# A DeltaNet mixer's triangular substitution moved from GpSimd to VectorE, with the projections around it put in another order

## The chip, the cores and the metric

The kernel runs on one core of a Trainium2 chip. The metric is the device time of one execution in microseconds (us), the median of three runs. Engines are named as the profile names them: PE is TensorE's matmul and PEld its weight load, DVE is VectorE, ACT is ScalarE, POOL is GpSimd, SP is SyncE, whose queue issues nearly all DMAs.

## The reference

Two trunk layers of width 1024 work on 384 tokens, 128 of a prompt and 256 of a sample. Layer 0 mixes by two head groups side by side, HGRN2 and gated DeltaNet, 4 heads of 128 each and both directions; layer 1 is neighbourhood attention. Each layer ends with a squared-ReLU MLP, and every part has an adaptive shift, scale and gate ("modulation"). The part of layer 0's mixer that matters here, cut:

```python
q_a, f_fw, f_bw, i_a, g_a, qkv_b, g_b, a_fw, a_bw, b_fw, b_bw = _split(h @ w_in, _AB_SIZES)
qa = _heads(jax.nn.silu(q_a), H_A).astype(f32) * DK_A ** -0.5
f = lbh + (1.0 - lbh) * jax.nn.sigmoid(_heads(f_raw, H_A).astype(f32))      # HGRN2's gate
qkv = jax.nn.silu(_short_conv(qkv_b, conv_w))                               # DeltaNet: 5 taps
qb = _l2norm(...) * DK_B ** -0.5 ; kb = _l2norm(...)
# _gated_delta_chunked, per chunk:
kb = k * beta[..., None]
A = jnp.where(strict, jnp.einsum('bhntd,bhnsd->bhnts', kb, k) * L, 0.0)     # L: decays
T = jnp.eye(CHUNK, dtype=A.dtype) + A
u = lax.linalg.triangular_solve(T, v * beta[..., None], left_side=True, lower=True, unit_diagonal=True)
w = lax.linalg.triangular_solve(T, kb * jnp.exp(g)[..., None], left_side=True, lower=True, unit_diagonal=True)
attn = jnp.where(tri, jnp.einsum('bhntd,bhnsd->bhnts', q, k) * L, 0.0)
```

The kernel takes whole tiles of 128 tokens as DeltaNet's chunks. It inverts T: first the 32 x 32 blocks on the diagonal by substitution, then two doubling levels (32 to 64 to 128) by matmuls.

## The kernel before, in words

Tokens lie in three tiles of 128. Each fp32 product is made of three matmuls: a weight half is loaded ("raw", a ring of 3), rounded by ACT ("whi", 4), and its rest ("wlo", 4) subtracted by DVE, or by POOL for the halves that the table `ON_POOL` names (`split_w`, L210). The input projection is done in blocks of 256 columns, each of two such halves: f (HGRN2's forget gates), q (its queries), v (its values), c (what DeltaNet's conv takes), g (output gates). A block of f, q, c or g is 48 matmuls (L645 to L647), one of v 72 (L687 to L689).

The order of the program comes from a string, `STEPS`: letters name a block, or so many steps of three generators: h is HGRN2 (seven doubling levels over three tiles, each a round over PE, ACT and DVE), d is DeltaNet's levels, a is the modulation (loads "adr", two slots, and 4 matmuls a step). A scheduler then takes the instructions of the whole program, estimates when each could run, and fixes the order on each engine; an engine runs its list strictly in that order. The table `ORDER` with `behind()` can pin an instruction behind another that was marked. Tiles come from rings: when a ring is full, whoever next takes a slot waits until its last reader is done. The ring "sm4" has five slots.

DeltaNet before the levels: `gdn_prep` makes, for each tile and direction, the products of the keys, times the decays (L997), into `NT_`, and 24 copies (L1000) take the diagonal blocks out of it. `gdn_solve` transposes these (L1030, L1035), weights them by cd = beta/|k|^2 (L1033), and sends them through DRAM (L1038, L1039, L1043) to a layout with one block in each of 96 partitions. There the substitution runs on POOL: 31 steps, each a product (L1052) and a subtraction (L1053). The inverses go back (L1055, L1057), are transposed (L1059), and written into the diagonal of `NT_` by 8 copies (L1074). The levels multiply by cd where they need it (L1091, L1120).

Also touched: `evac_q` (L705, L706: query times its sigmoid), `evac_f` (L714, L715: the gate), `evac_conv` (first tap L933, four more L935, then a sum on POOL, L943, and a transpose on PE, L949), `gdn_attn` (L1010), HGRN2's first products (L746, L747), its mask (L748) and its levels (L757, L762, L769, L771, L780, L783).

Of the kernel before, what the change touches and what calls it, by code (L numbers as in the profile page):

```python
# [48 lines left out]
}  # L49
# [6 lines left out]
d f3 f1 f2 d q1 a2 q0 d h a2 h a h c4 h a d h3 d c5 h a2 d h v0 h d h d v1 a d h3  # L56
c0 h3 c1 h5 d2 h d2 h d h7 g0 g1 d m g2 g3 a3
# [7 lines left out]
ON_POOL = {1: (0, 1), "c5": (0,), "q0": (0,)}  # L65
# [41 lines left out]
class Trunk:  # L107
# [525 lines left out]
    def fm_block(self, src, hh, evac, key):  # L633
# [6 lines left out]
        for g in range(2):  # L640
            with self.behind(key, g):
                for n in range(2):
                    c = slice(n * P, (n + 1) * P)
                    for k in range(g * 4, g * 4 + 4):
                        nc.tensor.matmul(pg[n], whi(k)[:, c], hhi[:, k], start=(k == 0), stop=False)  # L645
                        nc.tensor.matmul(pg[n], whi(k)[:, c], hlo[:, k], start=False, stop=False)  # L646
                        nc.tensor.matmul(pg[n], wlo(k)[:, c], hhi[:, k], start=False, stop=(k == KT - 1))  # L647
# [29 lines left out]
    def tm_half(self, src, hh, evac):  # L677
# [3 lines left out]
        whi, wlo = self.split_w(self.slab(src.rearrange("(k p) n -> p k n", p=P), KT, 256), KT, 256)  # L681
        for t0, n in ((0, 2), (2, 1)):
            pg = self.ps([P, 2, 256], "acc")[:, 0:n]
            for t in range(t0, t0 + n):
                c = slice(t * P, (t + 1) * P)
                for k in range(KT):
                    nc.tensor.matmul(pg[:, t - t0], hhi[:, k, c], whi(k), start=(k == 0), stop=False)  # L687
                    nc.tensor.matmul(pg[:, t - t0], hlo[:, k, c], whi(k), start=False, stop=False)
                    nc.tensor.matmul(pg[:, t - t0], hhi[:, k, c], wlo(k), start=False, stop=(k == KT - 1))  # L689
# [39 lines left out]
    def hgrn_tile(self, t, Q, K):  # L729
# [17 lines left out]
        nc.vector.tensor_mul(Q[:, 1], q, G[:, 0])  # L747
# [102 lines left out]

# [71 lines left out]
    def evac_conv(self, n):  # L922
# [4 lines left out]
        def f(pg):  # L927
# [5 lines left out]
            nc.vector.tensor_scalar(acc, raw[:, 0:386], w(0), None, op0=ALU.mult)  # L933
# [23 lines left out]
    def gdn_scalars(self):  # L957
        nc = self.nc
        c = lambda n: self.mixc([P, NT, 4], n)
        s, r2 = c("knorm"), c("kr2")  # L960
# [8 lines left out]
        bc = lambda x: x.unsqueeze(2).broadcast_to([P, NT, 2, 4])
        nc.vector.tensor_mul(self.cv, dh(self.beta), bc(s))  # L970
        nc.vector.tensor_mul(self.cd, dh(self.beta), bc(r2))
        nc.vector.tensor_mul(self.cs, self.cd, dh(self.eg))

    def block(self, j):
        return self.blocks[:, j].rearrange("p (d t h c) -> p d t h c", d=2, t=NT, h=4)

    def gdn_prep(self):

        nc = self.nc
        self.NT_ = self.m12([P, NT, 2, 4, P])  # L980
        self.AT_ = self.m12([P, NT, 2, 4, P])
        self.NC = self.block(0)
        b4 = lambda x: x.unsqueeze(1).broadcast_to([P, 4, P])
        for t in range(NT):
# [3 lines left out]
            for d in range(2):  # L988
# [8 lines left out]
                nc.vector.tensor_mul(self.NT_[:, t, d], pk, L)  # L997
                for b in range(4):
                    r = slice(32 * b, 32 * b + 32)
                    nc.vector.tensor_copy(self.NC[r, d, t], self.NT_[r, t, d, :, r])  # L1000

    def gdn_attn(self):

        nc = self.nc
# [18 lines left out]

    def gdn_solve(self):

        nc = self.nc
# [12 lines left out]
        nc.sync.dma_start(s1[:, 1], N3)  # L1039
        A = self.sm4([96, 32, 32])  # L1040
        sy = lambda s, b: s[32 * b:32 * b + 32].rearrange("i d (m j) -> (d m) i j", j=32)
        for b in range(4):
            nc.sync.dma_start(A[24 * b:24 * b + 24], sy(s1, b))  # L1043
# [4 lines left out]
        e = nc.gpsimd
        for j in range(31):
            m, w = 31 - j, j + 1  # L1050
            t = pr.rearrange("p i j -> p (i j)")[:, :m * w].rearrange("p (i j) -> p i j", j=w)
            e.tensor_tensor(t, A[:, w:, j:j + 1].broadcast_to([96, m, w]), X[:, j:j + 1, :w].broadcast_to([96, m, w]), op=ALU.mult)  # L1052
            e.tensor_tensor(X[:, w:, :w], X[:, w:, :w], t, op=ALU.subtract)  # L1053
# [767 lines left out]
```

## Time and profile before

| | us |
|---|---|
| three runs | 1140.26, 1137.22, 1137.5 |
| median | 1137.5 |
| profiled execution, own time | 1139.19 |
| its span in the profile | 1137.3 |
| its mean granted TensorE clock | 0.983 |
| TensorE busy in the span | 1081.7 (95%) |
| VectorE, ACT, POOL busy | 762.3, 485.1, 277.2 |

Busy times are sums over the span. In rows of a timeline the first number is the start, the second the duration; in groups the numbers after the bar are the sum and the mean in ns, then the idle time before them and what ended it. Line numbers are those of the kernel in question; those of the changed kernel are larger by three up to about line 960, and L210 becomes L213, L739 L742, L748 L751.

### The profile page before, as it was taken

To read this page: it belongs to the slowest core of one execution; us is meant where nothing else is said; L and a number is where in the kernel's file an instruction comes from. 1 tells how busy PE (TensorE), PEld (TensorE's weight loads), DVE (VectorE), ACT (ScalarE), POOL (GpSimd) and SP (SyncE) were. 2 spreads that over 40 slices of the span, in tenths; PEclk is the share of its full clock that TensorE was granted. 3 is DMA by queue.
4 is the path that set the end of the run, shared out by engine and by line. 5 is a ranking of instruction groups with operands and counts; after the bars stand their busy time and mean duration, and the time that the engine had idled before them with its cause. 6 is when DMAs were issued, how large, how long until landed. Compare 5 with 4: busy or idle time off the path is not lost.

```text
span 1137.3 us, 17975 instructions
## 1 busy us (share of the span) xinstructions
PE 1081.7 (95%) x6853; PEld 937.8 (82%) x6853; DVE 762.3 (67%) x1188; ACT 485.1 (43%) x874; POOL 277.2 (24%) x295
## 2 busy tenths in 40 slices
PE   6989969999998999999999999999988999999998
PEld 3868857988986898888889788888668889998987
DVE  3678499995467698968887654878748773333333
ACT  4464333342445543433334444656636433333330
POOL 0054894231204011111112252324012011111102
PEclk9989989999998999999999999999989999999999
DMA  8953725333162687766674147566425764433301
GB/s 290 292 168 107 220 79 162 129 108 110 38 218 78 244 275 261 260 202 222 226 248 134 41 101 211 153 185 167 119 74 184 281 203 130 133 126 126 99 38 56
DMA packets 142091, 184.66 MB, mean 162 GB/s; under 512 B 36803, under 2 KB 113685, under 8 KB 142005
## 3 DMA queue, kind: packets, MB, share of 16 engines
q1 hardware_dynamic: 141685, 183.44, 51.0%
q8 instruction: 54, 0.88, 0.3%
q14 instruction: 32, 0.26, 0.1%
q10 hardware_dynamic: 320, 0.07, 0.0%
HBM read 171.53 MB, written 4.61 MB: 155 GB/s over the span
## 4 chain that ended last, share of the span: by engine, by line
PE 74%; DVE 7%; DMA 6%; POOL 6%; issue 2%; SPq 2%; ACT 2%; POOLq 0%; DVEq 0%; ACTq 0%
PE acc L1340 7%; PE acc L1341 7%; PE acc L1342 7%; PE tmp L1355 7%; PE tmp L1356 7%; PE tmp L1354 7%; POOL sm L1053 2%; POOL sm L1052 2%; PE po L1731 2%; DMA ada<-in_ada_w 2%; PE acc L646 2%; PE acc L645 2%; PE acc L647 1%; PE acc L672 1%; PE acc L673 1%
## 5 line engine op out<-in xcount | busy, mean ns | idle before, releaser
L210 DVE TENSOR_TENSOR wlo<-raw,whi 128x1024 fp32r<-128x1024 f32 x192 | 238.0, 1250 | 167.2 <-ACT whi L209 145.5
L209 ACT ACTIVATE whi<-raw 128x1024 fp32r<-128x1024 f32 x198 | 205.9, 1050 | 335.0 <-PE acc L1342 190.6
L1374 POOL TENSOR_TENSOR h<-h 128x384 f32<-128x384 f32 x56 | 69.5, 1242 | 424.9 <-ACT h L1371 423.7
L1341 PE MATMUL acc<-wlo,h 128*128 128x512 f32 x380 | 148.5, 391 | 0.1
L1340 PE MATMUL acc<-whi,h 128*128 128x512 f32 x380 | 146.0, 393 | 0.6 <-issue 0.6
L346 DVE SCALAR_TENSOR_TENSOR adc<-adr,scz,adc 128x1024 f32<-128x1024 f32 x98 | 128.5, 1342 | 10.3 <-DMA adr<-in_ada_w 10.1
L1342 PE MATMUL acc<-whi,h 128*128 128x512 f32 x380 | 121.2, 391 | 0.0
L1340 PEld LDWEIGHTS acc<-whi,h 128*128 128x128 f32 x380 | 71.2, 188 | 20.6 <-ACT whi L209 5.0
L1355 PE MATMUL tmp<-hyA,whi 128*128 128x384 f32 (+1 forms) x256 | 85.1, 333 | 2.2 <-DVE hyA L565 2.2
L1354 PE MATMUL tmp<-hyA,whi 128*128 128x384 f32 (+1 forms) x256 | 84.1, 334 | 3.0 <-DVE hyA L564 3.0
L1354 PE MATMUL tmp<-hyB,whi 128*128 128x384 f32 (+1 forms) x256 | 83.8, 329 | 1.2 <-DVE hyB L564 1.2
L1356 PE MATMUL tmp<-hyA,wlo 128*128 128x384 f32 (+1 forms) x256 | 84.8, 332 | 0.0
L1355 PE MATMUL tmp<-hyB,whi 128*128 128x384 f32 (+1 forms) x256 | 84.0, 329 | 0.7 <-DVE hyB L565 0.7
L1341 PEld LDWEIGHTS acc<-wlo,h 128*128 128x128 f32 x380 | 71.4, 188 | 14.3 <-DVE wlo L210 0.5
L1342 PEld LDWEIGHTS acc<-whi,h 128*128 128x128 f32 x380 | 71.0, 188 | 13.7
L1356 PE MATMUL tmp<-hyB,wlo 128*128 128x384 f32 (+1 forms) x256 | 82.1, 328 | 0.0
L645 PE MATMUL acc<-hyA,whi 128*128 128x384 f32 x208 | 74.1, 356 | 0.0
L646 PE MATMUL acc<-hyA,whi 128*128 128x384 f32 x208 | 71.4, 343 | 0.0
L647 PE MATMUL acc<-hyA,wlo 128*128 128x384 f32 x208 | 71.0, 342 | 0.0
L1375 DVE TENSOR_TENSOR h<-h,h 128x384 fp32r<-128x384 f32 (+2 forms) x72 | 37.8, 526 | 40.6 <-POOL h L1374 39.8
L1354 PEld LDWEIGHTS tmp<-hyA,whi 128*128 128x128 f32 x256 | 48.7, 191 | 4.4 <-ACT km L560 3.4
L1355 PEld LDWEIGHTS tmp<-hyA,whi 128*128 128x128 f32 x256 | 49.3, 192 | 3.3 <-DVE hyA L565 2.4
(454 smaller groups left out, 2357.7 us busy)
## 6 DMA issues: line engine op xcount, KB each, us to landing
raw<-in_w_mlp SPq DMA_DIRECT2D x128, 512.0 KB, 3.8
adr<-in_ada_w SPq DMA_DIRECT2D x80, 512.0 KB, 4.7
raw<-in_w_in_ab SPq DMA_DIRECT2D x34, 512.0 KB, 4.7
ada<-in_ada_w SPq DMA_DIRECT2D x32, 256.0 KB, 5.5
raw<-in_w_qkv_na SPq DMA_DIRECT2D x32, 256.0 KB, 3.8
raw<-in_w_out_ab SPq DMA_DIRECT2D x8, 512.0 KB, 4.5
m<-gs SPq DMA_DIRECT2D x8, 512.0 KB
raw<-in_w_qkv_na SPq DMA_DIRECT2D x8, 512.0 KB
```

The costliest lines, as they stand in the source:

```text
L209: self.nc.scalar.activation(hi, x, AF.Copy)
L210: (eng or self.nc.vector).tensor_tensor(lo, x, hi.bitcast(F32), op=ALU.subtract)
L346: nc.vector.scalar_tensor_tensor(acc[v], raw, s[v], acc[v], op0=ALU.mult, op1=ALU.add)
L645: nc.tensor.matmul(pg[n], whi(k)[:, c], hhi[:, k], start=(k == 0), stop=False)
L646: nc.tensor.matmul(pg[n], whi(k)[:, c], hlo[:, k], start=False, stop=False)
L647: nc.tensor.matmul(pg[n], wlo(k)[:, c], hhi[:, k], start=False, stop=(k == KT - 1))
L1340: nc.tensor.matmul(pg, shi, w2hi(n)[:, o], start=start, stop=False)
L1341: nc.tensor.matmul(pg, shi, w2lo(n)[:, o], start=False, stop=False)
L1342: nc.tensor.matmul(pg, slo, w2hi(n)[:, o], start=False, stop=last)
L1354: nc.tensor.matmul(pg[n], w1hi(k)[:, c], hhi[:, k, tc_], start=(k == 0), stop=False)
L1355: nc.tensor.matmul(pg[n], w1hi(k)[:, c], hlo[:, k, tc_], start=False, stop=False)
L1356: nc.tensor.matmul(pg[n], w1lo(k)[:, c], hhi[:, k, tc_], start=False, stop=(k == KT - 1))
```

## The change

The substitution's 62 operations run on VectorE, over 112 partitions (one direction in partitions 0 to 47, the other from 64). One direction's blocks are turned end for end by a copy with a negative stride ahead of it, and turned back behind it. The diagonal blocks are fetched by DMA straight from `NT_` (four to DRAM, eight from there) and the inverses written by DMA straight back into it (eight to DRAM, one for the levels, four into `NT_`): 25 DMAs where 11 were. The 24 and the 8 copies, two transposes and two products by cd are gone. The keys' products take cd at once: 24 operations of 128 x 128 (`weigh`) for 6 of 128 x 512, in `gdn_prep` and again in `gdn_attn`; the products by cd in the levels become ACT copies, and the small vectors cv and cs are replaced by 1/|k|, eg and cu. The query's product goes to POOL (behind an ACT copy), the gate and the conv's first tap go to ACT. More halves are split on POOL: half of q1, both of v0 and v1, half of c4 (before: half of c5 and of q0). In `STEPS` the queries and values stand right behind the gates, ahead of HGRN2; an "a!" is pinned behind the block ahead of it, HGRN2's levels behind the substitution, and the transpose of the inverses behind HGRN2's first products. The last modulation steps are pinned behind the last gate block.

On POOL, the stretch around the substitution, before (wlo is a split half, sm tiles are of the ring sm4, km is HGRN2's 1 - f):

```order
L996 TENSOR_TENSOR m_121_750<-m_121_750,tri 128x512 x4
L210 TENSOR_TENSOR wlo_1282<-raw_1277,whi_1281 128x1024
L1046 MEMSET sm_139_846 96x1024
L1047 MEMSET sm_139_846 96x32
L1052 TENSOR_TENSOR sm_140_847<-sm_138_841,sm_139_846 96x31
L1098 MEMSET sm_203_1345 32x12x32
L1098 MEMSET sm_207_1391 32x12x32
L1053 TENSOR_TENSOR sm_139_846<-sm_139_846,sm_140_847 96x31
L1052 TENSOR_TENSOR sm_140_847<-sm_138_841,sm_139_846 96x60
```

and now:

```order
L1103 MEMSET sm_236_1626 32x12x32
L742 TENSOR_TENSOR km_1491<-x 128x512
L742 TENSOR_TENSOR km_1514<-x 128x512
L742 TENSOR_TENSOR km_1537<-x 128x512
L213 TENSOR_TENSOR wlo_1308<-raw_1303,whi_1307 128x1024
L213 TENSOR_TENSOR wlo_1312<-raw_1305,whi_1311 128x1024
L1103 MEMSET sm_240_1672 32x12x32
L710 TENSOR_TENSOR hyB_647<-hyB_647,cv_1209 128x3x128
L710 TENSOR_TENSOR hyB_647<-hyB_647,cv_1213 128x3x128
L213 TENSOR_TENSOR wlo_1404<-raw_1399,whi_1403 128x1024
L710 TENSOR_TENSOR hyB_647<-hyB_647,cv_1287 128x3x128
L213 TENSOR_TENSOR wlo_1408<-raw_1401,whi_1407 128x1024
```

wlo_1308 and wlo_1312 are the halves of the first value block, wlo_1404 and wlo_1408 those of the second. The second L1103 takes the sixth tile of a ring of five; the first of the five is the matrix A that the substitution reads (sm_137 below). On VectorE, around HGRN2's first products, before:

```order
L706 TENSOR_TENSOR hyB_647<-cv_1342,acc_1290 128x3x128
L746 TENSOR_TENSOR hq_1437<-hyB_647,m_102_649 128x512
L747 TENSOR_TENSOR hq_1437<-hyB_647,m_102_649 128x512
L746 TENSOR_TENSOR hq_1438<-hyB_647,m_102_649 128x512
L747 TENSOR_TENSOR hq_1438<-hyB_647,m_102_649 128x512
L746 TENSOR_TENSOR hq_1439<-hyB_647,m_102_649 128x512
L747 TENSOR_TENSOR hq_1439<-hyB_647,m_102_649 128x512
L748 TENSOR_TENSOR hyB_647<-hg_1443,eye 128x4x32
```

and now, from the substitution's last step:

```order
L1059 TENSOR_TENSOR sm_140_827<-sm_137_824,sm_139_826 112x31
L1060 TENSOR_TENSOR sm_139_826<-sm_139_826,sm_140_827 112x31
L1053 COPY sm_138_825<-sm_139_826 48x1024
L749 TENSOR_TENSOR hq_1487<-hyB_647,m_102_649 128x512
L750 TENSOR_TENSOR hq_1487<-hyB_647,m_102_649 128x512
L749 TENSOR_TENSOR hq_1488<-hyB_647,m_102_649 128x512
L750 TENSOR_TENSOR hq_1488<-hyB_647,m_102_649 128x512
L749 TENSOR_TENSOR hq_1489<-hyB_647,m_102_649 128x512
L750 TENSOR_TENSOR hq_1489<-hyB_647,m_102_649 128x512
L1207 STREAM_TRANSPOSE hyB_645<-hyB_645 128x768
L213 TENSOR_TENSOR wlo_1727<-raw_1720,whi_1726 128x1024
L213 TENSOR_TENSOR wlo_1909<-raw_1904,whi_1908 128x1024
```

HGRN2's first products, which stood behind the query's, now stand behind the whole substitution, and its first level behind four operations of DeltaNet's (L1115) and later halves:

```order
L213 TENSOR_TENSOR wlo_2383<-raw_2378,whi_2382 128x1024
L1115 TENSOR_SCALAR m_120_747<-gd_1644 32x12x32
L938 SCALAR_TENSOR_TENSOR cv_1782<-cr_652,prm,cv_1782 128x386
L1115 TENSOR_SCALAR m_120_747<-gd_1658 32x12x32
L938 SCALAR_TENSOR_TENSOR cv_1782<-cr_652,prm,cv_1782 128x386 x2
L1115 TENSOR_SCALAR m_120_747<-gd_1690 32x12x32
L213 TENSOR_TENSOR wlo_2387<-raw_2380,whi_2386 128x1024
L938 SCALAR_TENSOR_TENSOR cv_1782<-cr_652,prm,cv_1782 128x386
L1115 TENSOR_SCALAR m_120_747<-gd_1704 32x12x32
L774 COPY_PREDICATED hyB_647<-lv,hg_1818 128x4x32
```

L774 is the first level's masked copy. The diff, cut:

```diff
+    ("step", "!"): ["block"],
+    "hgrn": ["solve"],
+    "solved": ["hq"],
 STEPS = """
-d f3 f1 f2 d q1 a2 q0 d h a2 h a h c4 h a d h3 d c5 h a2 d h v0 h d h d v1 a d h3
-c0 h3 c1 h5 d2 h d2 h d h7 g0 g1 d m g2 g3 a3
+f3 a! f1 f2 a! q1 a! q0 a! v0 a! v1 h3 d2! a! d c4 h a! d h c5 h a! d h3 d h d h a! d2 h3
+c0 h3 c1 h5 d2 h d2 h d h7 g0 g1 d m g2 g3 a3!
-ON_POOL = {1: (0, 1), "c5": (0,), "q0": (0,)}
+ON_POOL = {1: (0, 1), "q1": (0,), "q0": (0,), "v0": (0, 1), "v1": (0, 1), "c4": (0,)}
     def evac_q
-            nc.vector.tensor_mul(self.qa[:, :, h], s, pv)
+            nc.scalar.activation(self.qa[:, :, h], pv, AF.Copy)
+            nc.gpsimd.tensor_tensor(self.qa[:, :, h], self.qa[:, :, h], s, op=ALU.mult)
     def evac_f
-            nc.vector.tensor_scalar(self.G[:, :, d, h], s, self.lb1[:, h:h + 1], self.lb[:, h:h + 1],
-                                    op0=ALU.mult, op1=ALU.add)
+            nc.scalar.activation(self.G[:, :, d, h], s, AF.Identity, scale=self.lb1[:, h:h + 1], bias=self.lb[:, h:h + 1])
     def evac_conv
-            nc.vector.tensor_scalar(acc, raw[:, 0:386], w(0), None, op0=ALU.mult)
+            nc.scalar.activation(acc, raw[:, 0:386], AF.Copy, scale=w(0))
     def gdn_prep
-                nc.vector.tensor_mul(self.NT_[:, t, d], pk, L)
-                for b in range(4):
-                    r = slice(32 * b, 32 * b + 32)
-                    nc.vector.tensor_copy(self.NC[r, d, t], self.NT_[r, t, d, :, r])
+                self.weigh(self.NT_[:, t, d], pk, L, t, d)
+    def weigh(self, out, pk, L, t, d):
+        for h in range(4):
+            self.nc.vector.scalar_tensor_tensor(out[:, h], pk[:, h], self.cd[:, t, d, h:h + 1], L[:, h], op0=ALU.mult, op1=ALU.mult)
+    def diagonal(self, b):
+        r = slice(32 * b, 32 * b + 32)
+        return self.nt[r].rearrange("p d t h c -> p d (t h) c")[:, :, :, r]
     def gdn_solve
...
+        A, A0 = self.sm4([P, 32, 32]), self.sm4([P, 32, 32])
+        X = self.sm4([P, 32, 32])
+        pr = self.sm4([P, 32, 32])
...
+        for b in range(4):
+            nc.sync.dma_start(s1[rows(b)], self.diagonal(b))
+        for d, x in enumerate((A0, A)):
+            for b in range(4):
+                nc.sync.dma_start(x[part(b, d)], blocks(s1, b, d))
...
+        reverse(A, A0)
+        e, n = nc.vector, 112
         for j in range(31):
...
+            e.tensor_tensor(t, A[:n, w:, j:j + 1].broadcast_to([n, m, w]), X[:n, j:j + 1, :w].broadcast_to([n, m, w]), op=ALU.mult)
+            self.mark["solve"] = e.tensor_tensor(X[:n, w:, :w], X[:n, w:, :w], t, op=ALU.subtract)
+        reverse(A0, X)
+        for d, x in enumerate((A0, X)):
+            for b in range(4):
+                nc.sync.dma_start(blocks(s2, b, d), x[part(b, d)])
+        nc.sync.dma_start(XC, s2)
         for b in range(4):
+            nc.sync.dma_start(self.diagonal(b), s2[rows(b)])
     def gdn_levels
-            nc.vector.tensor_mul(pb[T], p[T], cd[T].broadcast_to([32, NT, 4, 32]))
+            nc.scalar.activation(pb[T], p[T], AF.Copy)
     def gdn_steps
+        with self.behind("solved"):
+            nc.vector.transpose(self.blocks[:, 1], self.blocks[:, 0])
```

More of the change, by code (lines that the diff above doesn't have):

```diff
@@ L646, in fm_block @@
                         nc.tensor.matmul(pg[n], whi(k)[:, c], hlo[:, k], start=False, stop=False)
-                        nc.tensor.matmul(pg[n], wlo(k)[:, c], hhi[:, k], start=False, stop=(k == KT - 1))
+                        self.mark["block"] = nc.tensor.matmul(pg[n], wlo(k)[:, c], hhi[:, k], start=False, stop=(k == KT - 1))
         for n in range(2):
@@ L675, in tm_parts, with tm_half @@
         return part
-    def tm_half(self, src, hh, evac):
+    def tm_half(self, src, hh, evac, pool=()):
         nc = self.nc
         hhi, hlo = hh
-        whi, wlo = self.split_w(self.slab(src.rearrange("(k p) n -> p k n", p=P), KT, 256), KT, 256)
+        whi, wlo = self.split_w(self.slab(src.rearrange("(k p) n -> p k n", p=P), KT, 256), KT, 256, pool=pool)
         for t0, n in ((0, 2), (2, 1)):
@@ L688, in tm_half @@
                     nc.tensor.matmul(pg[:, t - t0], hlo[:, k, c], whi(k), start=False, stop=False)
-                    nc.tensor.matmul(pg[:, t - t0], hhi[:, k, c], wlo(k), start=False, stop=(k == KT - 1))
+                    self.mark["block"] = nc.tensor.matmul(pg[:, t - t0], hhi[:, k, c], wlo(k), start=False, stop=(k == KT - 1))
             evac(t0, n, pg)
@@ L794, in hgrn_steps @@
             for x in g:
-                next(x)
+                with self.behind("hgrn"):
+                    next(x)
                 yield
@@ new lines, in gdn_solve @@
+        s1 = self.dp.tile([P, 2, 12, 32], F32, tag="s1", name="s1")
+        s2 = self.dp.tile([P, 2, 12, 32], F32, tag="s2", name="s2")
+        rows = lambda b: slice(32 * b, 32 * b + 32)
+        blocks = lambda s, b, d: s[rows(b), d].rearrange("i m j -> m i j")
+        part = lambda b, d: slice(64 * d + 12 * b, 64 * d + 12 * b + 12)
+        for b in range(4):
+            nc.sync.dma_start(s1[rows(b)], self.diagonal(b))
+        for d, x in enumerate((A0, A)):
+            for b in range(4):
+                nc.sync.dma_start(x[part(b, d)], blocks(s1, b, d))
@@ L1053, in gdn_solve @@
-            e.tensor_tensor(X[:, w:, :w], X[:, w:, :w], t, op=ALU.subtract)
-        for b in range(4):
-            nc.sync.dma_start(sy(s2, b), X[24 * b:24 * b + 24])
-        XC = self.block(0)
-        nc.sync.dma_start(f(XC), s2.rearrange("p d c -> p (d c)"))
-        XD = self.block(1)
-        nc.vector.transpose(f(XD), f(XC))
-        self.Xc = (XC[:, 0], XD[:, 1])
-        self.XTc = (XD[:, 0], XC[:, 1])
+            t = flat(pr)[:n, :m * w].rearrange("p (i j) -> p i j", j=w)
+            e.tensor_tensor(t, A[:n, w:, j:j + 1].broadcast_to([n, m, w]), X[:n, j:j + 1, :w].broadcast_to([n, m, w]), op=ALU.mult)
@@ new lines, in gdn_solve @@
+            self.mark["solve"] = e.tensor_tensor(X[:n, w:, :w], X[:n, w:, :w], t, op=ALU.subtract)
+        reverse(A0, X)
+        XC, XD = (self.blocks[:, j].rearrange("p (d m c) -> p d m c", d=2, c=32) for j in range(2))
+        for d, x in enumerate((A0, X)):
+            for b in range(4):
+                nc.sync.dma_start(blocks(s2, b, d), x[part(b, d)])
+        nc.sync.dma_start(XC, s2)
+        for b in range(4):
+            nc.sync.dma_start(self.diagonal(b), s2[rows(b)])
+        self.Xc = [XD[:, d].rearrange("p (t h) c -> p t h c", t=NT) for d in range(2)]
@@ L1069, in gdn_levels @@
         N = XT = self.NT_
-        cd = self.cd[:, :, d].unsqueeze(3)
         tag = "gd"
-        for b in range(4):
-            r = slice(32 * b, 32 * b + 32)
-            nc.vector.tensor_copy(XT[r, :, d, :, r], self.XTc[d][r])
         first = lambda o, L: slice(o, o + L)
@@ L1474, in layer0 @@
         for step in STEPS.split():
-            kind, n = step[0], int(step[1:] or 1)
+            kind, n = step[0], int(step[1:].strip("!") or 1)
             if kind in chains:
                 for _ in range(n):
-                    next(chains[kind], None)
+                    with self.behind("step", step[-1]):
+                        next(chains[kind], None)
             elif kind == "f":
```

68 lines of the change are left out of this document (24 added, 44 removed).

## The prediction

> **What bounds the kernel now.** I began with the page: who is busy, where TensorE's clock is low, and which chain ended last.
>
> ```profile
> span 1137.3 us, 17975 instructions
> PE 1081.7 (95%) x6853; PEld 937.8 (82%) x6853; DVE 762.3 (67%) x1188; ACT 485.1 (43%) x874; POOL 277.2 (24%) x295
> ...
> PE 74%; DVE 7%; DMA 6%; POOL 6%; issue 2%; SPq 2%; ACT 2%; POOLq 0%; DVEq 0%; ACTq 0%
> ```
>
> TensorE is busy for 95% of the span; only its idle time and low clock can be won. POOL's 6% of the last chain is the substitution. The windows show where the mixer loses time (columns: PE, PEld, DVE, ACT, POOL busy, then PE's granted clock, DMA share, GB/s).
>
> ```profile
> 100.00:160.00 60.00, 51.44 (x453) 43.95 (x452) 42.15 (x52) 22.47 (x31) 43.28 (x51) 0.96 0.54 172
> 160.00:265.00 105.00, 99.71 (x1245) 87.57 (x1245) 94.67 (x160) 38.30 (x68) 43.45 (x56) 0.97 0.44 134
> 150.00:160.00 10.00, 5.00 (x78) 4.54 (x79) 10.00 (x12) 2.74 (x4) 9.37 (x11) 0.78 0.34 105
> 160.00:170.00 10.00, 8.61 (x139) 7.00 (x139) 10.00 (x13) 3.31 (x6) 9.37 (x10) 0.88 0.16 46
> ```
>
> From 100 to 265 us PE is idle 8.56 + 5.29 = 13.85 us and loses 0.04 x 51.44 + 0.03 x 99.71 = 5.05 us to the clock. VectorE (DVE) is itself busy 90% from 160 to 265. The waits of TensorE name two causes:
>
> ```profile
> PE tmp L949 <- POOL cv L943: 5.4, 2, 3.1
> ...
> PE hg L757 <- DVE hyB L748: 2.8, 1, 2.8
> PE hg L757 <- DVE hyB L771: 2.4, 2, 1.4
> ```
>
> L949 waits for POOL, where the conv's L943 stands in line with the substitution; L757 waits for HGRN2's levels on VectorE. The substitution's ends:
>
> ```profile
> 112.95 2.10 SPq L1043 DMA_DIRECT2D sm<-s  x4
> 117.38 0.25 POOL L1052 TENSOR_TENSOR sm<-sm,sm 96x31 f32<-96x31 f32 x1 [5.71 <-DMA sm<-s]
> 180.30 0.58 POOL L1053 TENSOR_TENSOR sm<-sm,sm 96x31 f32<-96x31 f32 x1
> 189.53 1.60 PE L1086 MATMUL gd<-hyB,m 32*32 32x32 f32 x48
> ```
>
> It runs from 117.4 to 180.9 (63.5 us), and DeltaNet's first level follows at 189.5.
>
> **The substitution moves.** Durations for VectorE and POOL, by group and from the timeline:
>
> ```profile
> L210 DVE TENSOR_TENSOR wlo<-raw,whi 128x1024 fp32r<-128x1024 f32 x32 | 42.9, 1347 | 24.2 <-ACT whi L209 19.8 <-PE ada L326 4.2
> L780 DVE TENSOR_TENSOR hq<-hq,m 128x512 f32<-128x512 f32 x21 | 17.9, 851 | 0.0
> L1000 DVE COPY hyB<-m 32x128 f32<-32x128 f32 x24 | 7.3, 304 | 0.4
> L997 DVE TENSOR_TENSOR m<-hg,m 128x512 f32<-128x512 f32 x6 | 4.1, 685 | 0.1
> L815 DVE SCALAR_TENSOR_TENSOR m<-hq,m,hg 128x128 f32<-128x128 f32 x8 | 2.2, 343 | 2.7 <-PE hg L836 2.7
> ...
> L210 POOL TENSOR_TENSOR wlo<-raw,whi 128x1024 fp32r<-128x1024 f32 x3 | 7.9, 2618 | 12.0 <-ACT whi L209 12.0
> L739 POOL TENSOR_TENSOR km<-x 128x512 f32<-128x512 f32 x3 | 3.8, 1274 | 0.0
> ...
> 91.61 0.18 DVE L971 TENSOR_TENSOR cd<-beta,kr 128x24 f32<-128x24 f32 x1
> 91.83 1.29 DVE L972 TENSOR_TENSOR cs<-cd,eg 128x24 f32<-128x24 f32 x1
> 95.73 1.30 POOL L996 TENSOR_TENSOR m<-m,tri 128x512 f32<-128x512 f32 x1 [0.19 <-ACT m L995]
> 134.27 1.10 POOL L1052 TENSOR_TENSOR sm<-sm,sm 96x231 f32<-96x231 f32 x1
> 134.81 3.44 DVE L747 TENSOR_TENSOR hq<-hyB,m 128x512 f32<-128x512 f32 x1
> 135.33 2.38 POOL L210 TENSOR_TENSOR wlo<-raw,whi 128x1024 fp32r<-128x1024 f32 x1
> ```
>
> Start: the keys' weighting is now 24 x 343 ns = 8.2 us where 24 copies and 6 products took 11.4, and its last piece can follow POOL's mask, which ended at 97.03: 97.03 + 4 x 0.343 = 98.4. SyncE then issues four DMAs and, behind one weight load, eight. By the row of four (issued from 112.95, landed before 117.38: 4.4 us, of which 2.1 is issue): first stage, issued at about 100, landed 104.5; second, twice the issue, 4.2 + 2.3, landed about 111.1; the reversing copy of 1024 elements, 0.5 to 1.3 us, taken as 0.7. I take 111.8 for the start, 5.6 us sooner than before. If the small pieces go slower it is 117.4 again.
>
> Length: 24 elements take 0.18 us, 512 take 0.685, so one element is 1.04 ns, the fixed part 0.155 and, with the 0.04 to the next start at 91.83, 0.19. There are 62 operations and 2 x 5456 = 10912 elements: 62 x 0.19 + 11.4 = 23.1 us. One weight split (L210: 1.35 with the company in its mean, taken as 1.2 without) stands among them: 24.3 us.
>
> Company: L971 and L972 have one shape, but L972, beside a POOL operation of 1.3 us, took 1.29 against 0.18. L747 took 3.44 instead of 0.69: it began inside POOL's L1052 and ended when POOL's L210 did. So a two-input VectorE operation waits out a whole POOL operation here. In the substitution's time POOL has three L739 (1.27 each) and the two splits of the first value block (2.38 each): 8.6 us. The substitution then ends at 111.8 + 24.3 + 8.6 = 144.7; with no such hold, at 136.1.
>
> [...] If it were instead a shared rate, the L780 mean against its undisturbed 0.68 would apply (0.851/0.68 = 1.25, so 23.1 x 0.25 = 5.8 us) and the end would be 141.9, the wait below 2.8 us shorter.
>
> **The wait that replaces it.** On POOL the second zeroing of L1103 (0.4 us) takes over the ring slot of the matrix that the substitution reads, so it waits for 144.7. Behind it stand, in order, two query products (L710, 128x384: three quarters of L739's 1.27, so 0.96 and a gap, 0.98 each), the first split of the second value block, another L710 and the second split. First split ready: 144.7 + 0.4 + 1.96 + 2.38 = 149.4, take 149.9 with the gaps; second 153.3. TensorE comes there early:
>
> ```profile
> 109.70 1.07 PE L326 MATMUL ada<-adr,scz 128*32 128x512 f32 x8
> ...
> 130.79 0.34 PE L647 MATMUL acc<-hyA,wlo 128*128 128x384 f32 x1
> ...
> 166.35 0.28 PE L687 MATMUL acc<-whi,hyA 128*128 128x256 f32 x1
> 166.47 0.28 PE L688 MATMUL acc<-whi,hyA 128*128 128x256 f32 x1
> ```
>
> The second query block ended at 131.0 behind the same five blocks; with an earlier front (1.5 us, below) and modulation behind its blocks rather than before them (2 us) that is about 127.7. Modulation 1.1 (the L326 row), then 72 matmuls spaced 0.12 (the two L687 rows) = 8.6, and modulation again: the second value block begins at about 138, and ends at 160.3 with its waits. Its wait is 149.9 - 138 = 11.9, and about 2 more for the second half: **14 us**. Bounds: 2.9 (substitution over at 136.1) and 20 (start at 117.4). [...] Its low clock costs what the slices behind the present hole show: 5.00 x 0.22 + 8.61 x 0.12 = 2.1 us.
>
> **What else moves.** Query products, gates, the conv's first tap and DeltaNet's level copies go to ACT and POOL. ACT is 43% busy and covers its part; uncovered it would be 0.5 us an item. In the front TensorE waits twice on the conv:
>
> ```profile
> PE tmp L949 <- POOL m L944: 1.2, 1, 1.2
> PE tmp L949 <- ACT cv L954: 1.2, 1, 1.2
> ```
>
> The shorter VectorE chain there may remove these: 0 to 2.4, taken as 1.5 gained. DeltaNet's levels come at about 162 instead of 189.5 (from 144.7 eight DMAs, 6.5 by the row of four; two more and the one that the levels read, about 5 with its landing; then VectorE's products, to 158.5, and its transpose, 1 us; the rest is the way to TensorE). Nothing of it waits at TensorE if the value block itself ends at 160.3.
>
> HGRN2 pays. Its first product L749 now stands on VectorE behind the substitution and behind POOL's last L710 (about 154), and its first level behind four L1115 and weight splits: about 178.5, where it was 152. What VectorE then has to do up to HGRN2's last level is, in the groups of 152 to 265 us of before:
>
> ```profile
> L935 DVE SCALAR_TENSOR_TENSOR cv<-cr,prm,cv 128x386 f32<-128x386 f32 x29 | 21.3, 735 | 0.2
> ...
> L210 DVE TENSOR_TENSOR wlo<-raw,whi 128x1024 fp32r<-128x1024 f32 x13 | 16.6, 1284 | 1.1 <-ACT whi L209 0.9
> L769 DVE TENSOR_TENSOR x<-x,m 128x512 f32<-128x512 f32 x19 | 15.4, 816 | 0.1
> L771 DVE COPY_PREDICATED hyB<-lv,hg 128x128 f32<-128x128 uint8 (+1 forms) x21 | 8.8, 420 | 0.5 <-PE hg L762 0.4
> L783 DVE TENSOR_TENSOR m<-m 128x512 f32<-128x512 f32 (+5 forms) x18 | 8.4, 472 | 0.0
> ```
>
> All 21 L771, 21 L780 and 18 L783 (35.1), 18 of the L769 (14.7), 23 conv taps (16.9), 8 splits (10.3) and about 6 of DeltaNet's: 83 us at these prices, 261.5. At undisturbed ones (0.69 for each operation of 512 elements, by L997) some 10 us less, 251.5. TensorE has, from 132 on, this:
>
> ```profile
> 132.00:265.00 133.00, 120.10 (x1520) 105.72 (x1517) 122.47 (x187) 47.84 (x84) 69.85 (x80) 0.96 0.42 130
> ```
>
> 120.1 less the clock's 4.8 (0.04 of it) and less 144 value matmuls at 0.12 leaves 98 us behind 160.3, so 258 to 259. The level waits are what VectorE is later: 0 to, with the 10.3 us of idle that VectorE has from 160 to 265 besides, 13. I take 3, by the 83 us; the present waits, the two L757, are 5.2.
>
> The last modulation step moves into the output projection, where each load of two ring slots must land:
>
> ```profile
> adr<-in_ada_w SPq DMA_DIRECT2D x80, 512.0 KB, 4.7
> ```
>
> Of such a landing the products between two loads hide a part that no row of before shows: 0 to 4.7, taken as 1.5.
>
> **The sum.** Against the profiled execution's own 1139.2 (span 1137.3, 1.9 around it; its time is 1.7 over the median): gone 13.85 + 5.05 + 1.5 = 20.4; added 14 + 2.1 + 3 + 1.5 = 20.6. The difference is +0.2, so 1139.4 for such an execution and **1137 to 1138 at the median; I say 1137**.
>
> **The rivals.** *Faster: no hold.* VectorE's short operations slip between POOL's, the substitution ends at 136.1, the split is ready at 140.9: wait 2.9, no clock lost. Sum: 20.4 - 2.9 - 3 - 1.5 = 13 gained, **1124.5**. For it: the many L1000 took their 0.30 beside POOL's masks with one input each. Against: L747, L972.
>
> *Slower: VectorE becomes the bound from 178.5.* To its 83 us come the 10.3 us that it now waits for TensorE's round trips: to 271.8, 12.9 behind TensorE, 9.9 more than I summed: **1147**. For it: 90% busy already, and HGRN2 began its levels 26 us sooner and still ended near 251. Against: POOL's long work is over by then. It decides once HGRN2's first level comes later than about 178.
>
> *The change doesn't do what it says: the blocks land no sooner.* Twenty-five DMAs replace eleven; if the second stage lands at 117.4, all of the wait chain shifts by 5.6: **1143**. For it: 128-byte pieces and a queue shared with weight loads. Against: 4.4 us for the row of four, whose pieces are as small. [...]
>
> **How the numbers follow.** My forecast has 0.34 (own range 1131 to 1142), no hold 0.30, VectorE the bound 0.28, late landing 0.08. A measurement of this kernel tells 0.3%, 3.4 us, from no change. Of the forecast's 0.34, 0.07 lies below that, 0.20 inside, 0.07 above; no hold is faster whole; of the bound 0.05 is inside and 0.23 above; of the late landing 0.02 and 0.06. Together faster 0.37, same 0.27, slower 0.36. The range leaves a tenth at each end, in the tails of the first two rivals: 1122 to 1150.
>
> **What would show it.** Right: VectorE's L1059 from about 112 to 144; POOL's L1103 waiting for it; PE's L692 waiting 10 us or more on POOL's split; L1091 near 162; HGRN2's first L774 near 178; few idle microseconds from 165 to 260. The hold shows in L1059/L1060 rows far over 0.45 us beside POOL's L742 and L213 (the old L739 and L210). Wrong: a value-block wait under 5 us, level waits on VectorE over 8 in all, or idle slices in the output projection over 5.

## The result, and the profile after

The changed kernel takes 1153.27 us (median of four runs, 1151.74 to 1155.6) where the kernel before took 1137.36 beside it: 1.0142 times as long, 95% interval 1.011 to 1.0173. It is slower by 16 us; the forecast was no change, 1137 us, and its range ended at 1150.

The page of the changed kernel:

```profile
span 1149.9 us, 17993 instructions
PE 1074.9 (93%) x6853; PEld 932.5 (81%) x6853; DVE 745.2 (65%) x1214; ACT 500.7 (44%) x906; POOL 250.2 (22%) x243
...
PE 69%; DVE 8%; DMA 5%; issue 4%; SPq 2%; POOL 2%; ACT 1%; DVEq 0%; POOLq 0%; ACTq 0%
```

Its windows (stretch, length, then busy times):

```profile
100.00:160.00 60.00, 39.12 (x242) 33.08 (x241) 38.41 (x74) 18.91 (x27) 24.65 (x16) 0.83 0.61 156
160.00:265.00 105.00, 99.52 (x1397) 88.26 (x1396) 82.55 (x140) 48.59 (x87) 28.50 (x32) 0.99 0.40 127
...
137.00:157.00 20.00, 0.27 (x3) 0.06 (x1) 10.47 (x24) 1.11 (x2) 11.58 (x8) 0.56 0.55 127
```

GpSimd has left the last chain (6% to 2%), as the change does it, and from 160 to 265 us TensorE is no idler than before (5.5 us against 5.3) at a better clock (0.99 for 0.97). But between 100 and 160 us it is idle 20.9 us where it was idle 8.6, at a granted clock of 0.83: from 137 to 157 it is busy for 0.27 us. Its waits say for what (in total, times, longest):

```profile
PE ada L329 <- DMA adr<-in_ada_w: 19.9, 1, 19.9
PE tmp L952 <- ACT cv L957: 4.5, 1, 4.5
PE hg L765 <- DVE hyB L774: 4.1, 2, 3.6
...
PE hg L983 <- ACT cv L718: 2.0, 1, 2.0
```

Not a split half of the second value block, but the modulation step that stands ahead of that block waits, for its load. The timelines of TensorE and of SyncE's queue (start, duration in us):

```profile
127.38 1.07 PE L329 MATMUL ada<-adr,scz 128*32 128x512 f32 x8
...
157.12 3.06 PE L329 MATMUL ada<-adr,scz 128*32 128x512 f32 x8 [19.85 <-DMA adr<-in_ada_w]
```

SyncE's timeline there:

```profile
117.85 0.82 SPq L326 DMA_DIRECT2D adr<-in_ada_w  x2
...
142.81 4.57 SPq L1066 DMA_DIRECT2D s<-sm  x8
...
151.79 1.21 SPq L326 DMA_DIRECT2D adr<-in_ada_w  x2
```

What SyncE waited for (in total, times, longest):

```profile
SPq L1066 <- DVE sm L1060: 21.5, 1, 21.5
```

In SyncE's list the eight transfers back (L1066) stand ahead of that step's two loads (L326). They wait 21.5 us for the substitution, and with them waits all that is queued behind: the loads go out at 151.79, though their two slots had been free since about 128.5, and TensorE, which reached the step at 137.3, goes on at 157.1. The forecast's own wait is there too, and of the forecast size, but covered. GpSimd's and VectorE's timelines:

```profile
110.59 3.95 POOL L742 TENSOR_TENSOR km<-x 128x512 f32<-128x512 f32 x3 [1.67 <-ACT x L740]
115.27 5.58 POOL L213 TENSOR_TENSOR wlo<-raw,whi 128x1024 fp32r<-128x1024 f32 x2 [0.74 <-ACT whi L212]
143.01 0.85 POOL L1103 MEMSET sm<- 32x384 f32 x1 [22.16 <-issue]
145.84 2.34 POOL L213 TENSOR_TENSOR wlo<-raw,whi 128x1024 fp32r<-128x1024 f32 x1
149.09 2.34 POOL L213 TENSOR_TENSOR wlo<-raw,whi 128x1024 fp32r<-128x1024 f32 x1
```

VectorE's timeline there:

```profile
112.41 0.93 DVE L1059 TENSOR_TENSOR sm<-sm,sm 112x31 f32<-112x31 f32 x1 [1.52 <-DMA sm<-s]
113.37 1.23 DVE L1060 TENSOR_TENSOR sm<-sm,sm 112x31 f32<-112x31 f32 x1
116.17 2.43 DVE L1059 TENSOR_TENSOR sm<-sm,sm 112x87 f32<-112x87 f32 x1
118.63 2.32 DVE L1060 TENSOR_TENSOR sm<-sm,sm 112x87 f32<-112x87 f32 x1
...
141.28 0.25 DVE L1059 TENSOR_TENSOR sm<-sm,sm 112x87 f32<-112x87 f32 x1
142.59 0.19 DVE L1060 TENSOR_TENSOR sm<-sm,sm 112x31 f32<-112x31 f32 x1
```

The substitution runs from 112.4 to 142.8 and four of its operations are held beside GpSimd (2.43 us where the same shape takes 0.25). GpSimd's first split of the second value block ends at 148.2 and the second at 151.4: 12 and 9 us before TensorE begins the block, at 160.1.

Where the time is lost, by places that both profiled executions pass (their spans differ by 12.6 us, not 16: that of before took 1139.19, more than the median, that of after 1151.74, the shortest of its four): the output projection begins at 327.8 instead of 322.6 and lasts 46.4 us instead of 37.4; the MLP's first product comes at 377.2 instead of 363.1, 14.1 us late, and 1.5 us of that come back by the end.

### The profile page after: what moved, and what is told of

Read it like the earlier page. It is cut to its first block, busy times and chain, and to the rows that moved or that the text cites. A ratio compares the mean times of both kernels' runs of the same rounds, so it can differ in the third digit from the quotient of the medians.

```text
span 1149.9 us, 17993 instructions
## 1 busy us (share of the span) xinstructions
PE 1074.9 (93%) x6853; PEld 932.5 (81%) x6853; DVE 745.2 (65%) x1214; ACT 500.7 (44%) x906; POOL 250.2 (22%) x243
## 4 chain that ended last, share of the span: by engine, by line
PE 69%; DVE 8%; DMA 5%; issue 4%; SPq 2%; POOL 2%; ACT 1%; DVEq 0%; POOLq 0%; ACTq 0%
PE tmp L1362 7%; PE tmp L1363 7%; PE tmp L1361 7%; PE acc L1347 7%; PE acc L1349 7%; PE acc L1348 7%; PE acc L675 2%; PE acc L676 2%; PE acc L677 2%; PE po L1739 2%; PE acc L648 1%; PE acc L649 1%; DMA adr<-in_ada_w 1%; PE acc L650 1%; DVE wlo L213 1%
## 5 line engine op out<-in xcount | busy, mean ns | idle before, releaser
L213 DVE TENSOR_TENSOR wlo<-raw,whi 128x1024 fp32r<-128x1024 f32 (+1 forms) x187 | 230.7, 1243 | 164.6 <-ACT whi L212 152.8
L648 PE MATMUL acc<-hyA,whi 128*128 128x384 f32 x208 | 71.7, 345 | 1.0 <-ACT hyB L709 1.0
L649 PE MATMUL acc<-hyA,whi 128*128 128x384 f32 x208 | 70.5, 339 | 0.0
```

What stands on the lines that cost most here:

```text
L213: (eng or self.nc.vector).tensor_tensor(lo, x, hi.bitcast(F32), op=ALU.subtract)
```

## The experiments

Theory A: SyncE's queue makes the loss, since a load that TensorE needs stands behind transfers that wait for the substitution. Theory B: GpSimd's line makes it, as forecast.

**e1**, the zeroing of L1103 on VectorE, so that GpSimd's splits no longer stand behind the substitution:

```diff
-        nc.gpsimd.memset(X[S, :, :, loc(T)], 0.0)
+        nc.vector.memset(X[S, :, :, loc(T)], 0.0)
```

> Only the two zeroings L1103 go from POOL to VectorE (there the second stands behind the substitution anyway), so that POOL's line with the second value block's splits no longer waits for the substitution. Theory A (the queue of SyncE: the modulation load that TensorE needs ahead of the second value block stands behind L1066, which waits for the substitution): POOL's splits are ready by about 130, but L329 still waits 19 to 20 us for its load and the time stays at 1153, within 3. Theory B (the forecast's own step: POOL's line sets the wait): the wait shrinks by 10 to 14 and the time falls to 1139 to 1143.

1162.46 us, 1.0216 (1.0193 to 1.024): 9.2 us slower than the change. Its waits and SyncE's timeline; then GpSimd's and VectorE's:

```profile
PE ada L329 <- DMA adr<-in_ada_w: 28.8, 1, 28.8
```

SyncE's timeline there:

```profile
151.88 4.61 SPq L1066 DMA_DIRECT2D s<-sm  x8
```

GpSimd's timeline there:

```profile
126.18 2.41 POOL L213 TENSOR_TENSOR wlo<-raw,whi 128x1024 fp32r<-128x1024 f32 x1 [3.00 <-ACT whi L212]
128.54 1.15 POOL L710 TENSOR_TENSOR hyB<-hyB,cv 128x384 f32<-128x384 f32 x1
```

VectorE's timeline there:

```profile
126.36 2.46 DVE L1060 TENSOR_TENSOR sm<-sm,sm 112x207 f32<-112x207 f32 x1
128.85 1.08 DVE L1059 TENSOR_TENSOR sm<-sm,sm 112x220 f32<-112x220 f32 x1
```

B falls: both splits of the second value block were ready by 132.2 and the wait grew. A's place was right and its figure, 1153, was not. GpSimd's freed work ran beside the substitution, each operation holding one of VectorE's to about its own length (2.46 us beside 2.41 and 1.08 beside 1.15 in the rows above), so the transfers back began 9.1 us later, TensorE waited 8.9 us longer and the kernel took 9.2 us more. One place sets all three.

**e2**, the modulation's loads issued by ScalarE instead of SyncE (`nc.scalar.dma_start` in `ada_quad`); **e3**, e1 and e2 together:

> Only the modulation's loads in the mixer (L326) are issued from ACT's queue instead of SyncE's. Theory A: L329 no longer waits; TensorE reaches the second value block at about 138 and waits there for POOL's split (ready at 148.2) about 10 us plus 1 to 2 for the second half, so 1153 falls by 7 to 11, to 1142 to 1146. Theory B alone (POOL's line): no change, 1153.

> Both edits. Theory A with POOL's line behind it: neither wait is left; the second value block runs from 138 to 147, and next TensorE waits for the transposed inverses at L1091 until about 154 (6 to 7 us). L1091 comes 14 to 16 us sooner than in the changed kernel (169.6), and if nothing else takes it back the time is 1138 to 1141. Rival (VectorE is the bound of the levels): HGRN2's last level stays near 261 and the time is 1147 to 1153.

1155.63 (1.0157, 1.0126 to 1.0187) and 1160.2 (1.0197, 1.0173 to 1.022; it has e1's hold besides, the transfers back begin at 150.4). The gain that A expected of both did not come; TensorE still waits 18.1 and 24.3 us at L329. ScalarE's timeline and SyncE's in e2:

```profile
150.08 0.98 ACTq L326 DMA_DIRECT2D adr<-in_ada_w  x2
151.39 0.60 ACT L1472 ACTIVATE hyB<-acc 128x512 f32<-128x512 f32 x1 [21.14 <-DMA s<-sm]
```

SyncE's timeline there:

```profile
144.06 4.66 SPq L1066 DMA_DIRECT2D s<-sm  x8
```

The load goes out at 150.08 on its own queue too, behind the transfers back. The instructions of e2, with what each waits for, tell why (from ScalarE's list and SyncE's):

```
L326 DMA adr_1391<-in_ada_w 128x1024 [waits DMAHW2_49,DMAHW0_49,PE_49]
L1066 DMA s_832<-sm_138_825 12x32x32 [waits DMAHW0_49]
L1066 DMA s_832<-sm_139_826 12x32x32 [waits DMAHW2_49]
```

In this program all DMAs, over both queues, take eight completion semaphores (DMAHW0 to DMAHW7) in turn, and the load waits for the DMA that had its semaphore (DMAHW2) before: a transfer back. So A has to be put wider: the load is late when it stands behind the way back in the program's order of DMAs, by SyncE's queue (151.79 in the change) as by ScalarE's (150.08 here). And now ScalarE's evictions waited 21.1 us behind it.

**e4**, the last modulation steps no longer pinned (`a3!` to `a3` at the end of `STEPS`):

> Only the pin of the last three modulation steps is taken off (the last word of the order string). If the output projection's 46.5 us (from its first to its last product; 37.4 before) come from the 24 modulation products in it and what waits for them: 38 to 42 us, L491 gone from the projection, and the total 2 to 6 us less than 1153, since the products' own 5 us go back ahead of it. If they are hidden anyway: no change.

1144.31 (1.0063, 1.0044 to 1.0082): 9 us less than the change (5.6 by the spans of the profiled executions, 1144.3 against 1149.9). The wait at L329 is 21.6 still; the projection lasts 37.7 us, as before the change. In the change 16 of these steps' 24 products (4.2 us), 0.6 us of waiting for a load and the products that spread the result (0.9) stood inside it.

**e5**, the 13 transfers back written behind the second value block's steps, so that the scheduler may put loads ahead of them; **e6**, e5 and e4 with the gates and the conv's first tap back on VectorE:

```diff
+        def back():
             for d, x in enumerate((A0, X)):
                 for b in range(4):
                     nc.sync.dma_start(blocks(s2, b, d), x[part(b, d)])
...
+        self.back()
         with self.behind("solved"):
             nc.vector.transpose(self.blocks[:, 1], self.blocks[:, 0])
```

> Only the place in the program where the inverses' thirteen DMAs back are written: behind the second value block (ahead of the transpose of the inverses) instead of at the end of the substitution, so that on SyncE's queue the loads for the step ahead of the second value block and for the block after it stand ahead of them. Theory A (SyncE's queue): the 19.9 us wait of L329 ahead of the second value block goes; that block ends near 147. Since POOL's splits and query products then run beside the substitution, it ends near 152, as in the run with the zeroings on VectorE (151.9); the next modulation load stands behind the DMAs back and lets TensorE wait at about 148 to 159. Net 1153 falls by 6 to 12, to 1141 to 1147. Rival (VectorE is the bound from here on): above 1149.

> The edit of e5, the last modulation steps unpinned (which alone gave 9 us), and the conv's first tap and the gate back on VectorE. If the three are independent: 1153 - 9 - (6 to 12) - (0 to 4 for the front, where TensorE is idle 7.3 us from 40 to 100 against 3.1 before) = 1128 to 1138. If what the front or the queue gives is taken back at a later wait: 1139 to 1145.

1142.62 (1.0027, 1.0002 to 1.0052) and 1142.64 (1.0044, 1.0025 to 1.0062). e5 takes 10.7 us off (6.7 by the spans of the profiled executions; its six runs spread from 1137.27 to 1145.02), within theory A's range, and neither value block waits; 12.4 us of waiting stand at the next modulation step instead. But e4's 9 us and the front's did not come on top. The waits and SyncE's timeline of e6:

```profile
PE ada L329 <- DMA adr<-in_ada_w: 10.8, 1, 10.8
```

SyncE's timeline there:

```profile
150.47 2.06 SPq L1068 DMA_DIRECT2D s<-sm  x4
152.63 1.13 SPq L326 DMA_DIRECT2D adr<-in_ada_w  x2
```

The wait has moved one modulation step on: the second value block now runs through, and the next step's load stands behind four of the transfers back. Why e4's gain did not add is not shown; the projection lasts 44.6 us here, not e4's 37.7, with no modulation product in it.

**e9**, e6 with that step written behind block c4 (`d2! a! d c4` to `d2! d c4 a!`); **e10**, e9 with the splits of q0, v0, v1 and c4 and the query's product on VectorE:

```diff
-ON_POOL = {1: (0, 1), "q1": (0,), "q0": (0,), "v0": (0, 1), "v1": (0, 1), "c4": (0,)}
+ON_POOL = {1: (0, 1), "q1": (0,), "v0": (), "v1": ()}
-            nc.scalar.activation(self.qa[:, :, h], pv, AF.Copy)
-            nc.gpsimd.tensor_tensor(self.qa[:, :, h], self.qa[:, :, h], s, op=ALU.mult)
+            nc.vector.tensor_mul(self.qa[:, :, h], s, pv)
```

> The kernel of e6 with one word of the order list moved: the modulation step that stood between HGRN2's first pieces after v1 and block c4 stands behind c4. In e6 the tensor engine waits 10.8 us at that step, for a load that SyncE issues at 152.6, behind four of the substitution's eight transfers back (150.5). Theory A (SyncE's queue alone makes this wait): the step behind c4 finds its load landed, the 10.8 us shrink to what c4's own weights make of it (one of its two slabs still stands behind the transfers back), 3 to 8 us; 1133 to 1138 us against e6's 1142.6. Rival B (the wait is only where the engine meets the late substitution; whatever comes next waits as long): the wait moves to c4 or to the levels' first product, at 10 us again: 1141 to 1145 us.

> e9 with less on GpSimd: the weight splits of blocks q0, v0, v1 and c4 and the product of the queries' gate are back on VectorE (one split of q1 stays on GpSimd). By the order of SyncE's queue both slabs of c4 then stand ahead of the transfers back. Seven splits of 1.23 us and four products of 0.55 us lengthen VectorE's line between 112 and 150 by some 11 us, and GpSimd's work beside the substitution (9.5 us in the changed kernel, with the lengthening of the products beside it) goes. Theory A (what the tensor engine meets behind v1 is loads held in SyncE's queue and buffers held by GpSimd's late splits): no wait over 3 us between 125 and 165; 1130 to 1135 us. Rival B (the substitution on VectorE is the line that everything meets; 11 us more on it come out again as a wait at q0, v0, or the first level): 1140 to 1148 us.

e9: 1139.18 (1.0026, 1.0008 to 1.0043), between the ranges of A and B. The wait at L329 is gone, and two others came, 6.7 and 5.0 us, inside c4 as B had it:

```profile
PE acc L650 <- DVE wlo L213: 6.7, 1, 6.7
...
PE acc L648 <- ACT hyB L1476: 5.0, 1, 5.0
```

VectorE's timeline there:

```profile
154.15 2.35 DVE L213 TENSOR_TENSOR wlo<-raw,whi 128x1024 fp32r<-128x1024 f32 x2
```

SyncE's timeline there:

```profile
156.06 2.78 SPq L207 DMA_DIRECT2D raw<-in_w_in_ab  x2
```

Only the second goes back to a load. The 6.7 us are for the second half of c4, which had been loaded and rounded by 136.6: its split stands in VectorE's list behind the substitution and HGRN2's first products and comes at 154.15. The 5.0 us are for an accumulator that c4 needs: ScalarE empties it (L1476) only behind the rounding of the next block's second half, and the load of that half goes out at 156.06, behind the eight transfers back; ScalarE waits for it until 161.9. So the substitution's end reached TensorE by VectorE's own line too, and not only by SyncE's queue. By the start of the projection nothing is gained (322.2 us, e6's 321.1): the 3.4 us show in the projection, which lasts 37.7 us again, and why is not shown.

e10: **1127.2, 0.9922 (0.9893 to 0.995) of the kernel before**, the fastest here. SyncE's timeline, VectorE's, and the window of 100 to 160:

```profile
143.40 0.80 SPq L326 DMA_DIRECT2D adr<-in_ada_w  x2
...
149.59 5.46 SPq L1067 DMA_DIRECT2D s<-sm  x8
```

VectorE's timeline there:

```profile
121.49 0.37 DVE L1060 TENSOR_TENSOR sm<-sm,sm 112x207 f32<-112x207 f32 x1
121.77 0.55 DVE L709 TENSOR_TENSOR hyB<-cv,acc 128x384 f32<-128x384 f32 x1
122.23 0.38 DVE L1059 TENSOR_TENSOR sm<-sm,sm 112x220 f32<-112x220 f32 x1
```

The window:

```profile
100.00:160.00 60.00, 56.24 (x421) 50.66 (x423) 46.75 (x92) 20.98 (x29) 4.38 (x4) 0.97 0.67 181
```

This is below the 1130 to 1135 of theory A. All loads that TensorE needs before 160 us now stand ahead of the way back, c4's splits stand between the substitution's steps (the last at 143.39), and TensorE has no wait over 3.8 us between 100 and 160. The substitution ends at 149.6, 7 us later than in the change, with the splits and products between its steps, and TensorE does not wait for it: DeltaNet's first level comes at 163.0 instead of 169.6. Which share of the 12 us against e9 is the splits' place and which the rest of the new list is not separated. (Between 108 and 150 us VectorE did eight splits and the four products there; GpSimd was busy 4.4 us from 100 to 160.)

**e11**, the same offload on the changed kernel alone; **e12**, e10 with the gates and the conv's first tap on ScalarE as in the change:

> The changed kernel with one edit of e10 alone: the weight splits of q0, v0, v1 and c4 and the product of the queries' gate on VectorE instead of GpSimd; the way back of the substitution and the modulation step stay where the change put them. By the order of SyncE's queue the load of that step then still stands behind the eight transfers back. Theory A (the load held in SyncE's queue is the cost, and the end of the substitution sets it): VectorE's line gets 11 us longer and loses the lengthening beside GpSimd, some 5 us; the substitution ends at 147 to 151 instead of 142.6, the wait at the modulation step grows from 19.9 to 24 to 28 us, and the time is 1157 to 1162 us, above the change's 1153.3, though the same edit was part of a kernel at 1127. Rival B (GpSimd's work beside the substitution is what the change pays for, and taking it away is what made e10 fast): at least half of the 15 us between e6 and e10 is seen here too, 1146 us or less.

> e10 with the front as the change has it: the first tap of the convolutions and the last step of the forget gates on ScalarE instead of VectorE. In the window 40 to 100 the tensor engine was busy 52.7 us in the changed kernel, 54.6 in e10 and 56.9 before. Theory A (the front costs time of its own, through waits for ScalarE's longer line): 2 to 5 us more than e10's 1127.2, 1129 to 1132 us, with waits for ScalarE of 6 us or more in that window. Rival B (the work taken off VectorE pays it back, since VectorE's line between 110 and 150 gets shorter by four gates of 0.67 us): 1124 to 1127.5 us.

e11: 1157.05 (1.019, 1.0162 to 1.0217). The time is in theory A's range by luck: the substitution ended at 141.5, not at 147 to 151, and the wait is in another place. Its waits, and VectorE's timeline:

```profile
PE acc L648 <- DVE hyB L709: 21.2, 1, 21.2
```

VectorE's timeline there:

```profile
141.55 0.81 DVE L1052 COPY sm<-sm 48x1024 f32<-48x1024 f32 x1
142.29 0.99 DVE L709 TENSOR_TENSOR hyB<-cv,acc 128x384 f32<-128x384 f32 x2
```

In e10 the query's products stand between the substitution's steps (121.77); here the scheduler put them behind its last (142.29), and TensorE waits for the accumulator that they empty. So e11 doesn't price the offload by itself: one edit gave a new list with another wait of 21 us.

e12: 1133.5 (0.9978, 0.9961 to 0.9996), 6.3 us more than e10 and above the 2 to 5 that theory A allowed. Before 100 us TensorE waits 4.5 and 2.0 us for ScalarE, as in the change, where e10's waits for it are 2.9 and 1.3. But at the start of the projection e12 is only 1.6 us behind (313.4 for 311.8); most of the 6.3 shows inside it, 43.6 us instead of 37.7, with waits of 2.7 us for ScalarE and 1.2 for VectorE. How the front comes to change the projection is not shown.

**e7 and e8**, the old order string with none of the new pins, the new layout and the keys' weights kept, the substitution on GpSimd (e7) or VectorE (e8), the query's product, gates and first tap on VectorE:

> The change without the move: the substitution on POOL (112 partitions), the old order string, the old table of POOL splits, no pins, the query product, gate and conv tap on VectorE as before; what stays is the keys' weighting, the copies and transposes that are gone, and the diagonal blocks by DMA. If the algebra and the DMAs are a gain that the order gave away: the substitution starts near 112 instead of 117 and the time is 1130 to 1136. If they are a loss of their own (24 narrow products for 6 wide ones, 25 DMAs for 11): above 1140. Worth nothing on the path: 1137.

> As e7, but the substitution on VectorE: the move alone, in the old order and without pins. If the order and its queue are the loss and not the engine: 1130 to 1142, no wait of TensorE for a modulation load above 5 us. If the engine is the loss (VectorE's line holds HGRN2 and the splits back): 1146 or more, with waits of TensorE on VectorE.

1161.42 (1.02, 1.0178 to 1.0221) and 1160.18 (1.0182, 1.0147 to 1.0218). Neither tells what it was for. They were meant to price the layout without the move. The waits and VectorE's timeline of e8:

```profile
PE ada L327 <- DMA adr<-in_ada_w: 12.7, 8, 5.0
```

VectorE's timeline there:

```profile
150.01 0.81 DVE L1051 COPY sm<-sm 48x1024 f32<-48x1024 f32 x1
150.85 1.02 DVE L707 TENSOR_TENSOR hyB<-cv,acc 128x384 f32<-128x384 f32 x2
```

The old string does not give the old order: the scheduler set the query's products behind the substitution (in e7 too, where VectorE stood idle meanwhile, 20.1 and 9.9 us at a stretch) and modulation products in a row in front, each pair waiting for its load. What the 25 transfers cost by themselves stays open, and so does what the move alone is worth: e10, the one kernel here that is faster than the one before, differs from it in more than the engine of the substitution.

## Why the prediction was wrong

**What stands ahead of the new wait, right.** The substitution began at 112.4 (forecast 111.8) and ended at 142.8 (144.7). Its own work was 24.4 us (24.3: the measured 30.4 less the four holds, 0.74 + 1.04 + 2.18 + 2.07 = 6.0); the hold was 6.0 instead of 8.6. The queries ended when forecast (127.4 for 127.7), and the first value block ended at 137.3 (with one step between, 138 for the second's start).

**The rivals.** "No hold" falls by the rows of 2.43 and 2.32 us, and e1 prices the hold from the other side: in its pairs VectorE's operation lasts about as long as GpSimd's beside it (2.46 and 2.41 us, 1.08 and 1.15). "VectorE the bound" is not seen: level waits are 4.7 us, not 12.9, and VectorE is busy 79% from 160 to 265, though its condition, a first level later than 178, came true (191.5). "Late landing" falls: 0.6 us late.

**The failed step** is in "The wait that replaces it": "Modulation 1.1 (the L326 row), then 72 matmuls ... and modulation again: the second value block begins at about 138, and ends at 160.3 with its waits." The second of these modulations was priced at its products. I had costed the 25 DMAs for when their data land, and L1066 for the way to the levels, but not what is queued behind L1066 on SyncE. The step waited 19.9 us for its load, began at a lower clock than the step before (granted 0.56 from 156.9 to 160.2 us, 1.00 from 127.3 to 128.5: its eight products took 3.06 us, the step before 1.07), and the block ended at 169.0: 8.7 us late. The forecast 14 us on GpSimd lay inside this wait, so the sign that was named for it, a wait of L692, did not show at all, and L1091 came at 169.6 for 162. That this step's wait is a cost of its own, e1 and e5 show from both sides: 8.9 us more of it came with 9.2 us more of time, and with it gone from this place the time fell by 10.7. The trace has the wait on SyncE's queue itself (L1066 waits 21.5 us on SPq), and the loads behind L1066 wait with it: L326 goes out at 151.79.

**Mis-sized.** The tail: 1.5 us forecast for the modulation inside the output projection, bounded by 4.7 for one landing; the projection lasts 9.0 us longer. I had counted the landings and left out the products (4.2 us of them inside it), which in the kernel before ran between 250 and 276 us, ahead of the projection; e4 prices the pin at 9 us, or 5.6 by the spans. The value block's 8.7 instead of 0 and 9.0 instead of 1.5 come to 16.2 us, where the profiled execution missed the forecast made for such an execution by 12.3 (1151.74 for 1139.4): places don't add up to the time, nor do the gains of e4 and e5 in e6. The front: the shorter VectorE chain was to gain 1.5; ScalarE's longer line made waits of 4.5 and 2.0 where 1.2 and 1.2 had been; in a kernel without the big wait the edit costs 6.3 us (e12), most of them not in the front. The level waits were 4.7 for 3; HGRN2's first level came at 191.5 for 178.5, behind the 19.9 us of waiting.

## What to carry to other kernels

When work moves to another engine, list for each queue, SyncE's first, what stands behind the instruction that waits for its end, and when each of those is needed; the last wait on TensorE is the latest of them, not the one that was looked at. Do the same for the engine that took the work: a split that stands behind it in VectorE's list held TensorE 6.7 us in e9. A DMA that waits for late data belongs behind every load needed before that data, in the program's order of DMAs and not only in its queue (e2's load, on ScalarE's queue, went out at 150.08, behind the transfers back from 144.06). And an order list is only what the scheduler starts from: after an edit, read the lists it made, since the same edit was worth 12 us in one (e10 against e9) and came with a loss in another (e11).

## What the runs showed of the hardware that I had not expected

GpSimd's steps were longer in company too (2.58 us for 1.52, start to start). With VectorE idle beside it, the substitution on GpSimd (e7) has these steps, where the kernel before, with VectorE busy beside it (7.96 us of the 8 from 144 to 152), has those (GpSimd's timelines):

```profile
136.19 0.64 POOL L1057 TENSOR_TENSOR sm<-sm,sm 112x256 f32<-112x256 f32 x1
136.91 0.73 POOL L1058 TENSOR_TENSOR sm<-sm,sm 112x256 f32<-112x256 f32 x1
```

GpSimd's timeline in the kernel before:

```profile
147.60 0.84 POOL L1052 TENSOR_TENSOR sm<-sm,sm 96x256 f32<-96x256 f32 x1
148.51 1.59 POOL L1053 TENSOR_TENSOR sm<-sm,sm 96x256 f32<-96x256 f32 x1
```

The whole ran from 109.7 to 155.2 in 45.5 us, with 7.6 us of other operations among them, against 63.5 with 10.2. By these rows GpSimd had been slow at it in part because of its company, not only by itself; no run changes the company alone. And a load issued from a second queue did not pass the first queue's transfers back (e2: out at 150.08, the transfers from 144.06), by the semaphores that the program shares out among both.
